# Decay input, sample rows and sample linear attention in plain fp32 over four column groups of TensorE

## The chip, the cores and the metric

One core of a Trainium2 chip runs the whole program. The metric is the device time of one execution in microseconds (us). TensorE is called PE (its weight loads PEld), VectorE DVE, ScalarE ACT, GpSimd POOL, and SyncE, which issues the DMAs, SP.

## The reference

One inference step of a decoder layer: a combined input projection feeds four heads of gated linear attention and a spatial-gating MLP, whose outputs share one output projection; a cross-attention over 256 memory tokens and a gated MLP with a causal convolution follow. There are 2048 prompt tokens and, beside them, 8 x 4 sample tokens that continue from a given state. All arrays are float32. The change touches the input projection and the linear attention:

```python
q, k, v, r, a, u, sv = split_cols(xn @ w_in)          # xn = rmsnorm(x, g_mix)
logg = log_sigmoid(a @ w_alpha + b_alpha) / 16        # a has 16 columns, logg 256
o, S = gla_chunked(q, k, v, logg, s0)                 # S_t = diag(exp(logg_t)) S_{t-1} + k_t^T v_t, o_t = q_t S_t
o = rmsnorm(o, g_gla_out) * silu(r)
sv = rmsnorm(gelu(sv), g_sgu)
```

## The kernel before

The prompt is worked in four blocks of 512 tokens (`s` is 0 to 3). The 32 sample tokens go through the mixer with block 1 (columns 512 to 543 of its tiles) and through the last MLP with block 2. `x` is kept with features on the partitions, in eight tiles `B.h[k]` of 128 x 544. A large product is done in three matmuls on split operands (`mm3`, lines 91 to 94): `split` makes of a fp32 tile a rounded part `hi` (ACT) and a remainder `lo` (DVE), both of the type fp32r, and the three products `hi hi`, `hi lo` and `lo hi` are summed in PSUM. `B.xs[k]` holds `hi` and `lo` of `x` times the gain `g_mix`; the scale of the norm (`B.xrs` by token, `B.xbc` broadcast) is applied when a result is taken from PSUM.

- `tm_steps` (line 674) makes products with tokens on the partitions: `sv` (profile name `t_ws`, line 816), `v` (`t_wv`) and `r` (`t_wr`). The eight feature tiles come in four weight units of two (step `j` = 0 to 3). In each step, each chunk `c` of 128 tokens takes six matmuls with the tokens as the stationary operand and 512 weight columns moving. In block 1 a fifth chunk holds the 32 sample tokens, also with 512 columns moving.
- `a_fn` (line 806) makes `a`, 16 columns wide, with features on the partitions: 16 matmuls of 32 stationary columns (`ap`, lines 812 and 813), on `wa1` (`hi` and `lo` of the weight side by side) and `wa2`. `gates` (line 900) multiplies it by `wal`, `w_alpha` twice and a row of `b_alpha` (`lgp`, plain fp32), and forms the log-sigmoid on ACT and DVE.
- `smp(p)` (line 1073) does the sample tokens' linear attention for a pair of heads: per head one matmul on the scores and eight on the given state (`ops`, lines 1079 and 1085), all summed in the same 32 PSUM rows; then `kvs` and the new state.
- `sample_steps` (line 1287) has a form that the change takes up: `sqp`, four plain fp32 matmuls of 32 stationary columns, each into another quarter of the PSUM partitions, and a product with `sum4` that adds the four quarters.

Weight tiles are loaded by `wload` into `wraw` tiles (five buffers), split into `whi` and `wlo` (five each), and asked for some five units ahead by `run`. What stands in which order on an engine is set by a scheduler when the program is built, from its own estimate of times; each engine then takes its instructions in that order. `acc` and `mps` are PSUM tiles, four buffers each.

Of the kernel before, what the change touches and what calls it, by code (L numbers as in the profile page):

```python
# [9 lines left out]
F32 = mybir.dt.float32  # L10
F32R = mybir.dt.float32r
# [26 lines left out]
def hymba_step_kernel(  # L38
# [31 lines left out]
    def acc(name):  # L70
        return accp.tile([128, 512], F32, tag="acc", name=name)
# [7 lines left out]
    def const(shape, name, dt=F32):  # L79
        return cp.tile(shape, dt, tag=name, name=name)  # L80
# [285 lines left out]
    pool.memset(sel[0:64, 0:1], 1.0)  # L366
    pool.memset(sel[64:128, 1:2], 1.0)

    cols_of = {}

    def load_cols(name, *vectors):
# [24 lines left out]
        nc.sync.dma_start(t, ap.partition_broadcast(128))  # L396
        return t

    wal = wa1 = wa2 = bsb = wsT = wss = None

    def late_constants():
        nonlocal wal, wa1, wa2, bsb, wsT, wss

        load_cols("b", ("gx", tiles_of(g_x)), ("gffn", tiles_of(g_ffn)),
                  ("cw", conv_w.rearrange("o j (k p) -> (o j k) p", p=128)), ("cb", tiles_of(conv_b)),
                  ("ggla", g_gla_out.rearrange("o h d -> (o h) d")), ("gsgu", g_sgu.rearrange("o h d -> (o h) d")))
        wal = const([33, 256], "wal")
        nc.sync.dma_start(wal[0:16, :], w_alpha[0])
        nc.sync.dma_start(wal[16:32, :], w_alpha[0])
        nc.sync.dma_start(wal[32:33, :], b_alpha)  # L410
        war = T_("war")
        war3 = war[:, :128].rearrange("p (k m) -> p k m", m=16)
        nc.sync.dma_start(war3, w_in[0, :, A0:A0 + 16].rearrange("(k p) m -> p k m", p=128))
        wa1 = const([128, 8, 32], "wa1", F32R)
        wa2 = const([128, 8, 32], "wa2", F32R)
        pool.memset(wa2[:, :, 16:32].bitcast(F32), 0.0)
        act.activation(wa1[:, :, 0:16], war3, AF.Copy)
        act.activation(wa2[:, :, 0:16], war3, AF.Copy)
        dve.tensor_tensor(wa1[:, :, 16:32], war3, wa1[:, :, 0:16].bitcast(F32), ALU.subtract)
# [12 lines left out]
        pool.tensor_copy(rep.rearrange("p (b i) -> p b i", i=4), ident[0:4, 0:4].unsqueeze(1).broadcast_to([4, 8, 4]))
        wss = const([NS, 4, NS], "wss")
        wssp = mps("wssp")
        pe.matmul(wssp[:NS, :16].rearrange("p (h i) -> p h i", h=4), rep, wsT[0:4, :, 0:4], start=True, stop=True)
        for h in range(4):
            dve.tensor_tensor(wss[:, h, :].rearrange("p (b i) -> p b i", i=4), blk3,
                              wssp[:NS, h * 4:(h + 1) * 4].unsqueeze(1).broadcast_to([NS, 8, 4]), ALU.mult)


        scd = state_conv[0].rearrange("b t f -> (b t) f")
        sctp = mps("sctp")
        for j in range(6):
# [229 lines left out]

    def tm_steps(w, m0, get_xs, sample, evac, name):

        ps = {}

        def fn(j, wu):
            xs = get_xs()
            wh, wl = wu  # L680
            for c in range(5 if sample else 4):
                n = 128 if c < 4 else NS
                cs = slice(c * 128, c * 128 + n)
                if j == 0:
                    ps[c] = acc(f"t_{name}{c}") if c < 4 else mps(f"t_{name}{c}")
                for kk in range(2):
                    k = 2 * j + kk
                    mm3(ps[c][:n], xs[k][0][:, cs], xs[k][1][:, cs], wh[:, kk], wl[:, kk], k == 0, k == 7)
                if j == 3:
                    evac(ps[c][:n], c, n)  # L690
        return [Step(lambda wu, j=j: fn(j, wu), [(w, 2 * j, 2, m0, 512, f"{name}{j}")]) for j in range(4)]

    def norm_in_steps(B):
# [81 lines left out]
    def proj_steps(B):  # L777
# [27 lines left out]

        def a_fn():
            B.aT = T_(f"aT{s}")
            pool.memset(B.aT[32:33, :T], 1.0)
            for ci, (c0, cw) in enumerate(chunks_of(sample)):
                ps = acc(f"ap{s}{ci}")  # L810
                for k in range(8):
                    pe.matmul(ps[:32, :cw], wa1[:, k], B.xs[k][0][:, c0:c0 + cw], start=k == 0, stop=False)
                    pe.matmul(ps[:32, :cw], wa2[:, k], B.xs[k][1][:, c0:c0 + cw], start=False, stop=k == 7)
                dve.tensor_tensor(B.aT[0:32, c0:c0 + cw], ps[:32, :cw], B.xbc[:32, c0:c0 + cw], ALU.mult)

        out = tm_steps(w, SV0, xs, sample, ev_tm("sv", lambda o, i, f: act.activation(o, i, AF.Gelu_apprx_tanh, scale=f)), f"ws{s}")
        out.append(Step(a_fn))
# [75 lines left out]
    def gla_steps(B):  # L893
# [6 lines left out]
        def gates():  # L900
            if sample:
                for p in range(2):
                    for i in range(2):
                        t = X(f"sg{p}{i}")
                        nc.sync.dma_start(t.rearrange("p (b v) -> p b v", b=4), sgd[:, 4 * i:4 * i + 4, p])
                        s0_of[p, i] = t
            lg = []
            for c2 in range(3 if sample else 2):
                n = 128 if c2 < 2 else NS
                wd = 512 if c2 < 2 else 256  # L910
                ps = mps(f"lgp{s}{c2}")
                for j in range(2 if c2 < 2 else 1):
                    c = 2 * c2 + j
                    pe.matmul(ps[:n, j * 256:(j + 1) * 256], B.aT[0:33, c * 128:c * 128 + n], wal, start=True, stop=True)
                t = T_(f"lgt{s}{c2}")
                act.activation(t[:n, :wd], ps[:n, :wd], AF.Abs)
                act.activation(t[:n, :wd], t[:n, :wd], AF.Exp, scale=-1.0)
                act.activation(t[:n, :wd], t[:n, :wd], AF.Ln, bias=1.0)
                o = U(f"lg{s}{c2}")
                dve.scalar_tensor_tensor(o[:n, :wd], ps[:n, :wd], 0.0, t[:n, :wd], ALU.min, ALU.subtract)  # L920
                lg.append(o[:, 0:256])
                if c2 < 2:
                    lg.append(o[:, 256:512])
            B.lg = lg
            B.P, B.qz, B.kt, B.eb, B.kms, B.b = {}, {}, {}, {}, {}, {}
# [147 lines left out]
        def smp(p):  # L1073
            s0 = [s0_of.pop((p, i)) for i in range(2)]
            ps = mps(f"ops{s}{p}")
            for hh in range(2):
                h = 2 * p + hh
                os_ = slice(hh * 128, (hh + 1) * 128)
                pe.matmul(ps[:NS, os_], B.P[h][:NS, SB:TM], B.v[4][:NS, h * 128:(h + 1) * 128], start=True, stop=False)
                qm = T_(f"qm{h}")  # L1080
                qm3 = qm[:, :256].rearrange("p (b i) -> p b i", b=8)
                pool.tensor_tensor(qm3, blkbc, B.qz[h][:, SB:TM].unsqueeze(1).broadcast_to([128, 8, NS]), ALU.mult)
                for bb in range(8):
                    sl = slice((bb % 4) * 128, (bb % 4 + 1) * 128)
                    pe.matmul(ps[:NS, os_], qm3[:, bb], s0[bb // 4][:, sl], start=False, stop=bb == 7)
            dve.tensor_copy(B.o[4][:NS, p * 256:(p + 1) * 256], ps[:NS, :256])
            for i in range(2):
                kv = mps(f"kvs{p}{i}")
                so = T_(f"so{p}{i}")
                for j in range(4):  # L1090
                    bb = 4 * i + j
                    sl = slice(j * 128, (j + 1) * 128)
                    for hh in range(2):
# [192 lines left out]

    def sample_steps():


        hr = [slice(h * NS, (h + 1) * NS) for h in range(4)]  # L1290

        def of_row(src, bb, name):

# [401 lines left out]
```

## Time and profile before

| | |
|---|---|
| median of three runs | 2878.52 us (2877.84 to 2882.15) |
| the profiled execution | 2882.3 us, its span 2880.3 us |
| PE busy | 2848.9 us |
| DVE, ACT, POOL busy | 1777.7, 1042.4, 615.6 us |
| moved by DMA | 625.47 MB, 217 GB/s over the span |
| mean granted clock of TensorE | 0.996 |

A row of a timeline gives the start, the duration, the engine and line, the output and inputs by the program's names, and how many instructions were merged into it; the duration of a matmul overlaps that of its neighbours, so what one occupies is read from the starts. One matmul in plain fp32 shows as two instructions. Rows of groups end with the busy time, the mean duration in ns, and the idle time ahead.

### The profile page before, as it was taken

How to read it: one execution, taken by the hardware profiler on the slowest of the kernel's cores; microseconds unless marked ns; L12 is line 12 of the kernel's file. 1: busy time of each engine (PE TensorE's matmuls, PEld its weight loads, DVE VectorE, ACT ScalarE, POOL GpSimd, SP SyncE). 2: the span in 40 equal slices, each digit the busy share in tenths (PEclk: the TensorE clock that was granted, in tenths of full speed). 3: DMA queues.
4: the chain of work that ended last, by engine and by line, in shares of the span. 5: the costliest groups of instructions: out<-in, count | busy, mean ns of one | idle time of the engine just before them, and what ended most of it. 6: DMA issues, size and time to landing. Idle time of an engine off the chain costs nothing.

```text
span 2880.3 us, 47363 instructions
## 1 busy us (share of the span) xinstructions
PE 2848.9 (99%) x18148; PEld 2519.9 (87%) x18148; DVE 1777.7 (62%) x3131; ACT 1042.4 (36%) x1890; POOL 615.6 (21%) x668
## 2 busy tenths in 40 slices
PE   8999999999999999999999999999999999999998
PEld 8888988887788898888888879899999888899998
DVE  7578468767657645555555773566666675474555
ACT  5635334333453423223124443422223533331221
POOL 1013112111112311222220221222221222132221
PEclk9999999999999999999999999999999999999999
DMA  9646579999932245877985214577776323567774
GB/s 311 203 151 219 186 252 328 332 325 339 341 105 61 66 141 186 303 273 277 326 313 200 74 45 165 195 256 260 258 265 213 106 66 106 191 249 266 275 283 177
DMA packets 359624, 625.47 MB, mean 217 GB/s; under 512 B 26683, under 2 KB 227326, under 8 KB 359400
## 3 DMA queue, kind: packets, MB, share of 16 engines
q1 hardware_dynamic: 359400, 622.46, 63.6%
q8 instruction: 144, 2.36, 0.3%
q14 instruction: 80, 0.66, 0.1%
HBM read 497.04 MB, written 125.31 MB: 216 GB/s over the span
## 4 chain that ended last, share of the span: by engine, by line
PE 89%; DVE 3%; DMA 3%; ACT 2%; issue 1%; POOL 1%; SPq 1%; DVEq 0%; POOLq 0%; ACTq 0%
PE d L92 5%; PE d L94 5%; PE d L93 5%; PE a_wo L92 2%; PE sc L94 2%; PE sc L93 2%; PE a_wo L93 2%; PE sc L92 2%; PE a_wo L94 2%; PE a_wx L94 2%; PE a_wx L93 2%; PE a_wx L92 2%; PE s L994 2%; PE t_wv L92 1%; PE t_wv L93 1%
## 5 line engine op out<-in xcount | busy, mean ns | idle before, releaser
L92 PE MATMUL d<-acth,whi_wd 128*128 128x512 f32 (+2 forms) x720 | 245.0, 340 | 0.1
L93 PE MATMUL d<-actl,whi_wd 128*128 128x512 f32 (+2 forms) x720 | 242.8, 337 | 0.0
L94 PE MATMUL d<-acth,wlo_wd 128*128 128x512 f32 (+2 forms) x720 | 242.8, 337 | 0.0
L1549 DVE TENSOR_TENSOR h<-d,h 128x512 f32<-128x512 f32 (+1 forms) x232 | 133.3, 581 | 145.0 <-PE d L94 144.8
L1488 POOL TENSOR_TENSOR c<-c,bc_f 128x512 f32<-128x512 f32 (+1 forms) x88 | 137.4, 1565 | 140.5 <-ACT c L1487 139.8
L94 PEld LDWEIGHTS d<-acth,wlo_wd 128*128 128x128 f32 x720 | 135.4, 188 | 15.7 <-issue 1.6
L92 PEld LDWEIGHTS d<-acth,whi_wd 128*128 128x128 f32 x720 | 135.5, 188 | 15.1 <-issue 1.2
L93 PEld LDWEIGHTS d<-actl,whi_wd 128*128 128x128 f32 x720 | 135.4, 188 | 14.6 <-issue 1.2
L1478 ACT ACTIVATE c<-g,colsb 128x512 f32<-128x512 f32 x88 | 71.7, 815 | 205.1 <-DVE g L1447 153.7
L94 PE MATMUL sc<-whi_qk,wol 128*128 128x256 f32 x512 | 144.4, 283 | 0.0
L92 PE MATMUL sc<-whi_qk,woh 128*128 128x256 f32 x512 | 144.1, 283 | 0.0
L93 PE MATMUL sc<-wlo_qk,woh 128*128 128x256 f32 x512 | 143.6, 282 | 0.0
L1510 POOL TENSOR_TENSOR c<-r_q_wup,c 128x512 f32<-128x512 f32 (+1 forms) x33 | 59.0, 1788 | 343.7 <-DVE r_q_wup L279 223.6
L1475 POOL COPY carry<-g 128x2 f32<-128x2 f32 x88 | 31.0, 353 | 435.3 <-DVE g L1447 433.2
L92 PE MATMUL a_wo<-ch,h_wo 128*128 128x512 f32 (+1 forms) x320 | 113.8, 359 | 5.4 <-DVE r L799 5.4
L987 POOL TENSOR_TENSOR e<-e,k 128x512 f32<-128x512 f32 (+1 forms) x48 | 69.2, 1442 | 223.6 <-DVE kr L983 160.9
L93 PE MATMUL a_wo<-cl,h_wo 128*128 128x512 f32 (+1 forms) x320 | 113.6, 356 | 0.2 <-POOL cl L85 0.2
L94 PE MATMUL a_wo<-ch,l_wo 128*128 128x512 f32 (+1 forms) x320 | 113.6, 355 | 0.0
L1479 DVE SCALAR_TENSOR_TENSOR c<-g,colsb,c 128x512 f32<-128x512 f32 x88 | 86.1, 978 | 30.5 <-ACT c L1478 30.0
L92 PE MATMUL a_wx<-pTh,whi_wx 128*128 128x512 f32 x256 | 101.0, 395 | 0.0
L93 PE MATMUL a_wx<-pTl,whi_wx 128*128 128x512 f32 x256 | 100.5, 393 | 0.0
L94 PE MATMUL a_wx<-pTh,wlo_wx 128*128 128x512 f32 x256 | 100.4, 392 | 0.0
(3355 smaller groups left out, 9463.6 us busy)
## 6 DMA issues: line engine op xcount, KB each, us to landing
whi_wd<-wd SPq DMA_DIRECT2D x66, 512.0 KB
wlo_wd<-wd SPq DMA_DIRECT2D x66, 512.0 KB
r_wo<-in_w_out_dram SPq DMA_DIRECT2D x32, 512.0 KB
whi_qk<-qkd SPq DMA_DIRECT2D x32, 512.0 KB
wlo_qk<-qkd SPq DMA_DIRECT2D x32, 512.0 KB
wlo_wx<-vod SPq DMA_DIRECT2D x32, 512.0 KB
whi_wx<-vod SPq DMA_DIRECT2D x32, 512.0 KB
r_wg<-in_w_gate_dram SPq DMA_DIRECT2D x22, 512.0 KB
```

The lines of the kernel that those rows point to most:

```text
L92: pe.matmul(ps, wh, xh, start=first, stop=False)
L93: pe.matmul(ps, wh, xl, start=False, stop=False)
L94: pe.matmul(ps, wl, xh, start=False, stop=last)
L987: pool.tensor_tensor(kl[:, :Tl], e[:, :Tl], B.k[p][:, :Tl], ALU.mult)
L994: pe.matmul(ps3[:, :, c * 64:(c + 1) * 64], kl[:, c * 128:(c + 1) * 128], kr3[:, :, c * 64:(c + 1) * 64], start=True, stop=True)
L1475: pool.tensor_copy(carry[:, f, :], g[:, SB:SB + 2])
L1478: act.activation(c[:, :SB], g[:, 2:SB + 2], AF.Identity, bias=cb, scale=w2)
L1479: dve.scalar_tensor_tensor(c[:, :SB], g[:, 1:SB + 1], w1, c[:, :SB], ALU.mult, ALU.add)
L1488: pool.tensor_tensor(c[:, :T], c[:, :T], B.fbc[:, :T], ALU.mult)
L1510: (dve, pool)[i].tensor_tensor(c[:, :T], q[i], c[:, :T], ALU.mult)
L1549: dve.tensor_tensor(B.h[m + mm][:, cs], ps[:, :cw], B.h[m + mm][:, cs], ALU.add)
```

## The change

1. The decay input `a` is made from `B.h` in plain fp32, feature tile `k` into column group `k % 4` (eight matmuls instead of 16); an ACT copy of all 128 rows replaces the scaled DVE copy, the sum over the four groups falls to `lgp` (`wal` now holds `w_alpha` four times), and the scale by token and the bias follow in a new DVE operation ahead of the log-sigmoid.
2. The sample rows of `sv`, `v` and `r` are made from the unsplit weights `raw` and `sxg` (sample columns of `x` times `g_mix`), four feature tiles at a time, each in its column group; after `j == 3` ACT copies the 128 x 512 result and one product with `sum4` adds the groups. The raw tile of a step is kept until that burst.
3. In `smp` the eight state products of a head go to four column groups; `ot` and `opt` add them.

```diff
+    hr = [slice(g * NS, (g + 1) * NS) for g in range(4)]
+    sxg = const([128, 8 * NS], "sxg")
...
-        wal = const([33, 256], "wal")
-        nc.sync.dma_start(wal[0:16, :], w_alpha[0])
-        nc.sync.dma_start(wal[16:32, :], w_alpha[0])
-        nc.sync.dma_start(wal[32:33, :], b_alpha)
+        wal = const([128, 256], "wal")
+        pool.memset(wal, 0.0)
+        for g in range(4):
+            nc.sync.dma_start(wal[g * NS:g * NS + 16, :], w_alpha[0])
+        bal = bvec(b_alpha.rearrange("o c -> (o c)"), 256, "bal")
...
+        wa = const([128, 8, 32], "wa")
+        pool.memset(wa, 0.0)
+        for k in range(8):
+            dve.tensor_scalar(wa[:, k, 0:16], war3[:, k], gcol("gmix", k), None, ALU.mult)
...
+        def spread(j):
+            if j == 1:
+                ps["q"] = mps(f"t_{name}q")
+            for k, raw in held:
+                pe.matmul(ps["q"][hr[k % 4]], sxg[:, k * NS:(k + 1) * NS], raw, start=j == 1, stop=j == 3)
+            held.clear()
+            if j == 3:
+                ps["t"] = T_(f"t_{name}t")
+                act.activation(ps["t"][:, :512], ps["q"], AF.Copy)
...
-            for c in range(5 if sample else 4):
+            if sample:
+                held.extend((2 * j + kk, raw[:, kk]) for kk in range(2))
+                if j % 2:
+                    spread(j)
+            for c in range(4):
...
+            if sample and j == 3:
+                ps[4] = mps(f"t_{name}4")
+                pe.matmul(ps[4][:NS], sum4, ps["t"][:, :512], start=True, stop=True)
+                evac(ps[4][:NS], 4, NS)
...
+            if sample:
+                dve.tensor_scalar(sxg[:, k * NS:(k + 1) * NS], B.h[k][:, SB:TM], gcol("gmix", k), None, ALU.mult)
...
                 for k in range(8):
-                    pe.matmul(ps[:32, :cw], wa1[:, k], B.xs[k][0][:, c0:c0 + cw], start=k == 0, stop=False)
-                    pe.matmul(ps[:32, :cw], wa2[:, k], B.xs[k][1][:, c0:c0 + cw], start=False, stop=k == 7)
-                dve.tensor_tensor(B.aT[0:32, c0:c0 + cw], ps[:32, :cw], B.xbc[:32, c0:c0 + cw], ALU.mult)
+                    pe.matmul(ps[hr[k % 4], :cw], wa[:, k], B.h[k][:, c0:c0 + cw], start=k < 4, stop=k >= 4)
+                act.activation(B.aT[:, c0:c0 + cw], ps[:, :cw], AF.Copy)
...
-                act.activation(t[:n, :wd], ps[:n, :wd], AF.Abs)
+                o = U(f"lg{s}{c2}")
+                for j in range(wd // 256):
+                    js = slice(j * 256, (j + 1) * 256)
+                    dve.scalar_tensor_tensor(o[:n, js], ps[:n, js], B.xrs[:n, 2 * c2 + j:2 * c2 + j + 1], bal[:n],
+                                             ALU.mult, ALU.add)
+                act.activation(t[:n, :wd], o[:n, :wd], AF.Abs)
...
-                    pe.matmul(ps[:NS, os_], qm3[:, bb], s0[bb // 4][:, sl], start=False, stop=bb == 7)
-            dve.tensor_copy(B.o[4][:NS, p * 256:(p + 1) * 256], ps[:NS, :256])
+                    pe.matmul(ps[hr[bb % 4], os_], qm3[:, bb], s0[bb // 4][:, sl], start=0 < bb < 4, stop=bb >= 4)
+            ot = T_(f"ot{p}")
+            dve.tensor_copy(ot[:, :256], ps[:, :256])
...
+            ps = mps(f"opt{s}{p}")
+            pe.matmul(ps[:NS, :256], sum4, ot[:, :256], start=True, stop=True)
+            dve.tensor_copy(B.o[4][:NS, p * 256:(p + 1) * 256], ps[:NS, :256])
```

The scheduler orders the program anew. On PE, in block 1's product `v`, the sample chunk of the first weight unit stood before like this (`t_wv_8610` is its PSUM tile, `xh` and `xl` the split `x`):

```order
L94 MATMUL t_wv_8596<-h_wv_8140,xl_1_7810 128x512
L92 MATMUL t_wv_8610<-h_wv_8140,xh_0_7805 32x512
L93 MATMUL t_wv_8610<-l_wv_8141,xh_0_7805 32x512
L92 MATMUL t_wv_8603<-h_wv_8140,xh_0_7805 128x512
```

and the same place has now, up to the second weight unit (`t_wv1q` is the PSUM tile of the four groups):

```order
L685 MATMUL t_wv1q<-r_wv_8136,sxg 32x512
L92 MATMUL t_wv_8591<-h_wv_8138,xh_0_7809 128x512
L93 MATMUL t_wv_8591<-l_wv_8139,xh_0_7809 128x512
L94 MATMUL t_wv_8591<-h_wv_8138,xl_0_7810 128x512
L92 MATMUL t_wv_8591<-h_wv_8138,xh_1_7814 128x512
L93 MATMUL t_wv_8591<-l_wv_8139,xh_1_7814 128x512
L94 MATMUL t_wv_8591<-h_wv_8138,xl_1_7815 128x512
L685 MATMUL t_wv1q<-r_wv_8136,sxg 32x512
L685 MATMUL t_wv1q<-r_wv_8251,sxg 32x512 x2
```

The sample matmuls moved out of the chunks into four new ones, of which one stands apart from the other three. On PE at the end of block 1's linear attention, ahead of its output projection, stood before:

```order
L1085 MATMUL ops_9566<-sg_8390,qm_9579 32x128 x4
L1085 MATMUL ops_9566<-sg_8392,qm_9579 32x128 x4
L1095 MATMUL kvs_9590<-v_8819,km_9456 64x128 x2
L1095 MATMUL kvs_9605<-v_8819,km_9457 64x128 x2
L865 MATMUL zp_9656<-wsT,sv_8150 128x128
```

and now stands:

```order
L1115 MATMUL ops_9539<-sg_8375,qm_9552 32x128 x4
L1126 MATMUL kvs_9564<-v_8799,km_9436 64x128 x2
L1126 MATMUL kvs_9579<-v_8799,km_9437 64x128 x2
L1133 MATMUL opt_9594<-ot_9562,sum_151 32x256
L685 MATMUL t_wr1q<-r_wr_8777,sxg 32x512 x2
L685 MATMUL t_wr1q<-r_wr_8995,sxg 32x512 x2
L685 MATMUL t_wr1q<-r_wr_9001,sxg 32x512 x2
L685 MATMUL t_wr1q<-r_wr_9231,sxg 32x512 x2
```

All eight sample matmuls of `r` moved behind the linear attention, so that its four raw weight tiles `r_wr` are in use up to there. On SP's queue the loads of the output projection's weights (`r_wo`) stood before:

```order
L102 DMA r_wo_9257<-in_w_out_dram 128x4x256
L102 DMA r_wo_9477<-in_w_out_dram 128x4x256
L102 DMA r_wo_9620<-in_w_out_dram 128x4x256
L857 DMA gsgub<-in_g_sgu_dram 32x512
L859 DMA out_dram<-svo 32x512
L102 DMA r_wo_9671<-in_w_out_dram 128x4x256
```

and now stand:

```order
L102 DMA r_wo_9237<-in_w_out_dram 128x4x256
L883 DMA gsgub<-in_g_sgu_dram 32x512
L885 DMA out_dram<-svo 32x512
L1131 DMA out_dram<-so_8963 128x4x128
L1376 DMA kc_12122<-in_cache_mem_k_dram 128x512
L1131 DMA out_dram<-so_8978 128x4x128
L1376 DMA kc_12124<-in_cache_mem_k_dram 128x512
L102 DMA r_wo_9457<-in_w_out_dram 128x4x256
```

The second of these loads moved behind two state outputs, and it and the three after it now each wait for the split of the load before.

More of the change, by code (lines that the diff above doesn't have):

```diff
@@ L397, in bvec @@
         return t
-    wal = wa1 = wa2 = bsb = wsT = wss = None
+    wal = wa = bal = bsb = wsT = wss = None
     def late_constants():
-        nonlocal wal, wa1, wa2, bsb, wsT, wss
+        nonlocal wal, wa, bal, bsb, wsT, wss
         load_cols("b", ("gx", tiles_of(g_x)), ("gffn", tiles_of(g_ffn)),
@@ L413, in late_constants @@
         nc.sync.dma_start(war3, w_in[0, :, A0:A0 + 16].rearrange("(k p) m -> p k m", p=128))
[L414 to L419, printed above, removed]
+        wa = const([128, 8, 32], "wa")
+        pool.memset(wa, 0.0)
+        for k in range(8):
+            dve.tensor_scalar(wa[:, k, 0:16], war3[:, k], gcol("gmix", k), None, ALU.mult)
         bsb = bvec(b_s.rearrange("o h i -> (o h i)"), 512, "bsb")
@@ L676, in tm_steps, with unit, load @@
         ps = {}
+        held = []
+        def spread(j):
[7 more added lines that the diff above has]
+                act.activation(ps["t"][:, :512], ps["q"], AF.Copy)
         def fn(j, wu):
             xs = get_xs()
-            wh, wl = wu
-            for c in range(5 if sample else 4):
-                n = 128 if c < 4 else NS
-                cs = slice(c * 128, c * 128 + n)
+            raw, wh, wl = wu
+            if sample:
[3 more added lines that the diff above has]
+            for c in range(4):
+                cs = slice(c * 128, (c + 1) * 128)
                 if j == 0:
-                    ps[c] = acc(f"t_{name}{c}") if c < 4 else mps(f"t_{name}{c}")
+                    ps[c] = acc(f"t_{name}{c}")
                 for kk in range(2):
                     k = 2 * j + kk
-                    mm3(ps[c][:n], xs[k][0][:, cs], xs[k][1][:, cs], wh[:, kk], wl[:, kk], k == 0, k == 7)
+                    mm3(ps[c], xs[k][0][:, cs], xs[k][1][:, cs], wh[:, kk], wl[:, kk], k == 0, k == 7)
                 if j == 3:
-                    evac(ps[c][:n], c, n)
-        return [Step(lambda wu, j=j: fn(j, wu), [(w, 2 * j, 2, m0, 512, f"{name}{j}")]) for j in range(4)]
+                    evac(ps[c], c, 128)
+            if sample and j == 3:
+                ps[4] = mps(f"t_{name}4")
+                pe.matmul(ps[4][:NS], sum4, ps["t"][:, :512], start=True, stop=True)
+                evac(ps[4][:NS], 4, NS)
+        def unit(j):
+            def load():
+                raw = wload(w, 2 * j, 2, m0, 512, f"{name}{j}")
+                return raw, *wsplit(raw, f"{name}{j}")
+            return load
+        return [Step(lambda wu, j=j: fn(j, wu), [unit(j)]) for j in range(4)]
     def norm_in_steps(B):
@@ L807, in a_fn @@
             B.aT = T_(f"aT{s}")
-            pool.memset(B.aT[32:33, :T], 1.0)
             for ci, (c0, cw) in enumerate(chunks_of(sample)):
@@ L913, in gates @@
                     c = 2 * c2 + j
-                    pe.matmul(ps[:n, j * 256:(j + 1) * 256], B.aT[0:33, c * 128:c * 128 + n], wal, start=True, stop=True)
+                    pe.matmul(ps[:n, j * 256:(j + 1) * 256], B.aT[:, c * 128:c * 128 + n], wal, start=True, stop=True)
                 t = T_(f"lgt{s}{c2}")
-                act.activation(t[:n, :wd], ps[:n, :wd], AF.Abs)
+                o = U(f"lg{s}{c2}")
[4 more added lines that the diff above has]
+                act.activation(t[:n, :wd], o[:n, :wd], AF.Abs)
                 act.activation(t[:n, :wd], t[:n, :wd], AF.Exp, scale=-1.0)
                 act.activation(t[:n, :wd], t[:n, :wd], AF.Ln, bias=1.0)
-                o = U(f"lg{s}{c2}")
-                dve.scalar_tensor_tensor(o[:n, :wd], ps[:n, :wd], 0.0, t[:n, :wd], ALU.min, ALU.subtract)
+                dve.scalar_tensor_tensor(o[:n, :wd], o[:n, :wd], 0.0, t[:n, :wd], ALU.min, ALU.subtract)
                 lg.append(o[:, 0:256])
@@ L1287, in sample_steps @@
     def sample_steps():
-        hr = [slice(h * NS, (h + 1) * NS) for h in range(4)]
         def of_row(src, bb, name):
```

## The prediction

> **What bounds the kernel now.** I read the page's busy table and chain first, then who TensorE (PE) waits for, then the stretches around block 1, which alone carries the 32 sample tokens.
>
> ```profile
> span 2880.3 us, 47363 instructions
> PE 2848.9 (99%) x18148; PEld 2519.9 (87%) x18148; DVE 1777.7 (62%) x3131; ACT 1042.4 (36%) x1890; POOL 615.6 (21%) x668
> PE 89%; DVE 3%; DMA 3%; ACT 2%; issue 1%; POOL 1%; SPq 1%; DVEq 0%; POOLq 0%; ACTq 0%
> ```
>
> PE is busy 2848.9 of 2880.3 us, so 31 us idle are left in the whole program, and 89% of the chain that ended last is PE. A matmul row taken from PE's queue shortens the span unless a wait opens in its place. The waits say where that is nearest:
>
> ```profile
> PE a_wo L92 <- DVE r L799: 5.4, 3, 2.2
> PE s L994 <- POOL e L987: 4.6, 4, 1.5
> 970.00:980.00 10.00, 10.00 (x77) 7.69 (x77) 5.65 (x11) 7.46 (x27) 5.19 (x3) 1.00 0.63 211
> 980.00:990.00 10.00, 8.65 (x63) 6.92 (x61) 6.80 (x18) 1.91 (x6) 6.57 (x5) 0.69 0.16 47
> 990.00:1000.00 10.00, 9.83 (x64) 9.32 (x64) 8.78 (x28) 5.91 (x10) 1.34 (x1) 0.80 0.20 60
> ```
>
> The first two rows are the longest recurring waits. The other rows are stretches (columns: PE, PEld, DVE, ACT, POOL busy, granted clock, DMA share, GB/s). Just ahead of block 1's out projection (`a_wo`) PE is idle 1.35 us of ten, and the clock falls to 0.69 and 0.80. Elsewhere in block 1 PE is full.
>
> **The prices.** A matmul's own duration overlaps its neighbours', so I price by start to start. First what goes:
>
> ```profile
> 805.40 0.39 PE L92 MATMUL t_ws<-h_ws,xh 128*32 128x512 f32 x1
> ...
> 806.79 0.38 PE L1589 MATMUL yp<-ident,h 128*128 128x128 f32 x2
> 106.70:110.45 3.75, 3.73 (x16) 1.64 (x16) 0.00 (x0) 1.00 1.07 352
> 822.36:826.44 4.08, 4.08 (x32) 3.47 (x32) 0.00 (x0) 1.00 0.27 68
> 976.45 1.94 PE L1085 MATMUL ops<-sg,qm 128*32 128x128 f32 x16
> 978.31 0.40 PE L1079 MATMUL ops<-v,P 32*32 32x128 f32 x2
> 978.64 1.93 PE L1085 MATMUL ops<-sg,qm 128*32 128x128 f32 x16
> 980.51 0.65 PE L1095 MATMUL kvs<-v,km 32*64 32x128 f32 x8
> ```
>
> - Sample rows of the token-major products: six split matmuls run from 805.40 to 806.79, 1.39 us, so the 24 of one product take 5.56 and the three products (`ws`, `wv`, `wr`) 16.7 us.
> - Decay input `ap`: 16 matmuls of 512 columns in 3.73 us in each of three blocks, and 32 of 272 columns in 4.08 in block 1: 15.3 us.
> - State term `ops`: 978.31 minus 976.45, and 980.51 minus 978.64, is 1.86 and 1.87 per head, four heads: 7.5 us.
>
> Removed: 39.5 us. What comes instead is plain fp32 over four column groups. The trace has that form (`sqp`, a sample projection), and it has plain fp32 over the full array (`lgp`); each fp32 matmul shows as two instructions:
>
> ```profile
> 1160.55 0.28 PE L93 MATMUL a_wup10S<-wul,wup10A 128*128 128x256 f32 x1
> 1160.67 0.28 PE L94 MATMUL a_wup10S<-wuh,wup10A 128*128 128x256 f32 x1
> 1160.88 1.07 PE L1311 MATMUL sqp<-r_sq,smpx 128*32 128x256 f32 x16
> 1161.88 0.39 PE L92 MATMUL a_wg11A<-w,wg11A 128*128 128x256 f32 x1
> 1162.10 0.29 PE L93 MATMUL a_wg11A<-w,wg11A 128*128 128x256 f32 x1
> 1162.23 0.28 PE L94 MATMUL a_wg11A<-w,wg11A 128*128 128x256 f32 x1
> 126.29 1.99 PE L914 MATMUL lgp<-wal,aT 33*128 33x256 f32 x8
> 128.21 0.50 PE L92 MATMUL a_wq<-xh,h_wq 128*128 128x512 f32 x1
> ```
>
> Four `lgp` matmuls of 256 columns take 1.92 us, 0.48 each. Eight `sqp` matmuls of 256 take 1.00 us, 0.125 each: the groups run side by side, 3.84 times faster. Around such a burst the start to start grows from 0.12 to 0.21 and from 0.13 to 0.22, so a burst costs 0.18 more at its edges; I take 0.2. Four neighbours of 512 columns stream what eight of 256 do: 1.0 us. One that stands alone takes 0.96.
>
> The Trainium skill, page "TensorE: Matmul & The Clock Gate", section "Measured speedup vs the span model", measured 3.07 for four tiles (packed by rows). Our trace has 3.84 for four column groups and decides; by 3.07 the 20.0 us of bursts below (edges apart) would be 25.0, an estimate.
>
> The Trainium skill, page "TensorEngine Tiling (Array Packing)", section "Key Properties", says that changing the tiling mode drains TensorE. That speaks against scattered bursts, and by it every piece pays; the rows agree, at 0.09 us per edge.
>
> **What is added on PE.**
> - Products: `ws` comes in two bursts of four, 2.0 us. `wv` stands in the order as one alone plus three, twice: 2 x (0.96 + 1.0) = 3.9. `wr` is one burst of eight, 2.0. Seven pieces of edges, 1.4. Each product ends with a 512-column fp32 sum over the groups, 0.96 plus edge 0.1: 3.2. Together 12.5 us.
> - `ap`: two blocks 2.0 each; block 3, where a transpose splits one off, 3.0; block 1 has 16 of 272 columns, 16 x 272 / 2048 = 2.1. Edges of five pieces 1.0. Together 10.1.
> - `ops`: 16 of 128 columns per pair of heads are 2048 columns, 1.0 us if the streaming limits; if one instruction cannot follow another faster than in `sqp` (16 in 1.00 us), 32 take 2.0. I take the middle, 1.5, since no row has this form at 128 columns; two pairs 3.0 (ends 2.0 and 4.0). Two 256-column sums, 0.48 + 0.1 each: 1.2. Together 4.2.
>
> Added 26.8, removed 39.5: PE's queue gets 12.7 us shorter. `lgp` streams the same 256 columns with 128 rows instead of 33 at the same start to start, so I price it at zero.
>
> **What is added elsewhere.** The decay's scale and bias move behind `lgp`: 17 vector operations of 128x256. The nearest row:
>
> ```profile
> L983 DVE SCALAR_TENSOR_TENSOR kr<-e,sel,q 128x256 f32<-128x256 f32 x104 | 46.4, 485 | 19.3 <-ACT e L975 15.9 <-ACT e L977 2.6 <-DMA out_dram<-so 0.8
> 840.00:850.00 10.00, 10.00 (x73) 9.14 (x72) 6.05 (x19) 9.76 (x14) 0.00 (x0) 1.00 0.36 106
> 20.00:30.00 10.00, 10.00 (x88) 10.00 (x87) 5.14 (x9) 4.65 (x8) 0.00 (x0) 1.00 1.13 302
> ```
>
> 8.2 us on DVE, some two per block, beside 96 queued `a_wq` matmuls that stand between `lgp` and its reader (840 to 850: PE full, DVE 60%). Cost zero; without that cover it would be the 2 us of a block. ACT is at 98% there, and takes the two `aT` copies from DVE; they stand before `lgp`, covered by `a_wk`. The eight scalings for `sxg` and the copies `t`, `ot` are under 1 us each and have matmuls queued behind them. At the start two DMAs more and a 128 KB broadcast of the bias enter a saturated stretch (20 to 30: DMA share 1.13, 302 GB/s), 0.4 us, while PE is full: between 0 and 1, I take 0.4.
>
> **The loads behind it.** A raw weight tile is now kept until the burst that reads it, instead of until its split. In `wr` all four are kept to the end, so of five buffers one is left, and the next loads (`r_wo`, on SP's queue) go through it one after the other: each waits for the split of the one before.
>
> ```profile
> 919.63 0.38 SPq L102 DMA_DIRECT2D r_wo<-in_w_out_dram  x1
> 920.50:921.00 0.50, 0.50 (x6) 0.50 (x6) 0.48 (x2) 0.00 (x0) 0.00 (x0) 1.00 0.47 70
> 922.00:922.50 0.50, 0.50 (x7) 0.48 (x6) 0.50 (x3) 0.02 (x1) 0.00 (x0) 1.00 0.96 338
> L84 ACT ACTIVATE h_wo<-r_wo x8: 1046/1058/1062, 935.8 to 1012.9; 128x1024 fp32r<-128x1024 f32 x8
> L85 DVE TENSOR_TENSOR l_wo<-r_wo,h_wo x8: 1202/1224/1227, 938.0 to 1014.0; 128x1024 fp32r<-128x1024 f32 x8
> ```
>
> A lone 512 KB load goes from 919.63 to 922.5, 2.9 us; with the splits 1.06 and 1.22 one turn takes 5.2. Four turns after the first split (938.0) end by 960, and `a_wo` starts at 988.9, so PE never lacks the weights. But ACT and DVE take instructions in order, and the splits now stand between the `e`, `kh` and `o` steps of the linear attention: each of four may hold them up by up to the 2.9 us of a load. I expect most of it covered by `t_wr` matmuls and take 1 us, ends 0 and 11.6.
>
> **The end of block 1.** The burst of `wr` (2.2), `opt` and the last sum come where PE idles 1.35 us, between `ops` and `a_wo`; I give 1 us back for that, ends 0 and 1.35. They also need PSUM buffers there.
>
> Sum: -12.7 + 0.4 + 1 - 1 = -12.3 us. On the profiled execution, 2882.3 us (span 2880.3), that is 2870.0; this execution lies 3.8 above the median of the three runs shown, 2878.52, so I predict 2866.2 us.
>
> **Rivals.**
> 1. Clock kept. These rows show where it halves:
>
> ```profile
> 988.90 0.57 PE L92 MATMUL a_wo<-ch,h_wo 128*128 128x272 f32 x1 [1.09 <-DVE r L799]
> 989.27 0.43 PE L93 MATMUL a_wo<-cl,h_wo 128*128 128x272 f32 x1
> ...
> 994.22 0.29 PE L92 MATMUL a_wo<-ch,h_wo 128*128 128x272 f32 x1
> 994.35 0.29 PE L93 MATMUL a_wo<-cl,h_wo 128*128 128x272 f32 x1
> ```
>
> The matmuls follow at 0.23 us until 994, then at 0.13. With dense bursts in the stretch before, the drop may not come: about half of the 5.2 us from 988.9, 2.6, and 1.5 from the `zp` ahead of it. Result -12.3 - 4.1 = -16.4, 2862. Against it: the waits ahead of `a_wo` (1.09) stay.
> 2. The splits hold up block 1's chain: with 7 to 11.6 us exposed instead of 1 the result is -6 to -2, about 2875. For it: DVE and ACT are in order; against it: DVE is only 57% busy at 970 to 980.
> 3. Slower: the column groups do not run side by side with 512 columns. The place is every burst. The bursts without their edges are 7.9 + 9.1 + 3.0 = 20.0 us; without overlap their 24 + 24 matmuls of 512 columns cost 0.96, the 16 of 272 0.51 and the 32 of 128 0.24, together 61.9, and the sum becomes +30, 2908. It decides from 20.0 + 12.3 = 32.3 us on, bursts 1.6 times as long as priced. Against it: `sqp`, same form, half the columns.
> 4. The overlap lies between: where the groups' streams hinder each other at 512 columns, bursts of 25 instead of 20 us give -7.3, 2871. `sqp` speaks against it, but at 256 columns. (That is the overlap of the Trainium skill's page "TensorE: Matmul & The Clock Gate", section "Measured speedup vs the span model"; no run here shows it.)
>
> **How the numbers follow.** Main case (-9 to -15) 55%; clock kept (-15 to -20) 13%; overlap between, or part of rival 2 (-6 to -9) 15%; rival 2 in full (within 6 us) 11%; slower by over 6 us 6%, half of it rival 3. 0.2%, 5.8 us, is what a measurement tells from no change. Faster 0.83, same 0.11, slower 0.06. The range goes from 2858, just beyond the clock case, to 2875, into rival 2; outside lie the slower cases and half of rival 2 above, and little below, some 14% in all.
>
> **What would show it.** `t_ws` of 128*32 with fp32r gone, `t_ws1q` in bursts of 1.0 us per four; `ap` near 2.0 us instead of 3.73; `ops` near 1 to 2 us per pair of heads instead of 3.7; PE's busy time shorter by some 12 us, its idle time near 31. Wrong: `t_wr1q` over 4 us, PE waits on `P`, `kh` or `o` in block 1, or a start of `a_wo` later than 12 us ahead of 988.9.

## The result and the profile after

The changed kernel takes 2865.24 us (median of five, 2863.78 to 2871.47) against 2879.53 us before (2877.84 to 2882.15): ratio 0.995, 95% interval 0.994 to 0.9961. The prediction was 2866.2 us, range 2858 to 2875, and a change of -12.3 us; measured are -14.3 us, with the interval -17.3 to -11.2. The sum came out near, but its gains and two of its losses were priced too low, as the profile shows. Two executions far off the others, 3739.79 us of the kernel before and 6203.86 us of `light_start`, are left out of the ratios below. The profiled execution after took 2871.47 us (span 2869.5), the slowest of the five. From its page: span, PE's busy time, the chain's shares.

```profile
span 2869.5 us, 47351 instructions
PE 2834.5 (99%) x18134; PEld 2504.1 (87%) x18134; DVE 1784.4 (62%) x3160; ACT 1044.4 (36%) x1896; POOL 613.9 (21%) x665
PE 91%; DVE 3%; ACT 2%; issue 1%; POOL 1%; DMA 1%; SPq 0%; DVEq 0%; POOLq 0%; ACTq 0%
```

From the list of what PE waited for (total us, times, longest):

```profile
PE a_wo L92 <- DVE r L827: 4.3, 2, 2.2
PE bp L960 <- DVE lg L950: 3.8, 2, 2.2
PE mkt L567 <- DVE mkf L558: 2.8, 2, 1.9
```

PE is busy 14.4 us less than before, where 12.7 were priced. But its idle time grew from 31.4 to 35.0 us. The wait of block 1's `a_wo` for `r` (1.09) is gone, and in its place stand two waits that before did not have: `bp`, the running sum of the decay `lg` and the next matmul after `a_wq`, waits for `lg`, and at the start `mkt`, which transposes the keys `mkf` of the memory tokens, waits for `mkf`.

The matmuls, from PE's timeline after (start, duration, ..., how many):

```profile
109.59 1.92 PE L839 MATMUL ap<-h,wa 128*32 128x512 f32 x16
111.44 0.98 PE L589 MATMUL wqp<-ident,r_wqf 128*128 128x128 f32 x7
112.19 0.47 PE L92 MATMUL a_wk<-xh,h_wk 128*128 128x512 f32 x1
...
127.09 1.89 PE L940 MATMUL lgp<-wal,aT 128*128 128x256 f32 x8
128.63 0.58 PE L92 MATMUL a_wq<-xh,h_wq 128*128 128x512 f32 x1
...
799.77 1.07 PE L685 MATMUL t_ws1q<-r_ws,sxg 128*32 128x512 f32 x8
800.76 0.50 PE L92 MATMUL t_ws<-h_ws,xh 128*128 128x512 f32 x1
...
909.04 0.65 PE L1115 MATMUL ops<-sg,qm 128*32 128x128 f32 x16
909.62 0.40 PE L1109 MATMUL ops<-v,P 32*32 32x128 f32 x2
909.95 0.64 PE L1115 MATMUL ops<-sg,qm 128*32 128x128 f32 x16
910.52 0.65 PE L1126 MATMUL kvs<-v,km 32*64 32x128 f32 x8
```

Four sample matmuls of 512 columns take 0.99 us (799.77 to 800.76; a fp32 matmul shows as two instructions). `ap` of block 0 takes 1.85. One head's eight state matmuls take 0.57 or 0.58, a third of the 1.86 before. `lgp` on 128 rows takes 1.54 from its start to `a_wq`; on 33 rows it took 1.92.

The new wait in block 1. Before, on PE and DVE, the same `lg` ended at 851.05, with `bp` at 854.01, so that 3.0 us of slack were left:

```profile
854.01 1.05 PE L930 MATMUL bp<-tri,lg 128*128 128x128 f32 x8
850.04 1.01 DVE L920 SCALAR_TENSOR_TENSOR lg<-lgp,lgt 128x512 f32<-128x512 f32 x2 [3.50 <-ACT lgt L918]
```

On PE, DVE and ACT after:

```profile
848.51 0.60 PE L960 MATMUL bp<-tri,lg 128*128 128x128 f32 x4
851.32 0.72 PE L960 MATMUL bp<-tri,lg 128*128 128x128 f32 x4 [2.20 <-DVE lg L950]
...
838.97 0.47 DVE L945 SCALAR_TENSOR_TENSOR lg<-lgp,xrs,bal 128x256 f32<-128x256 f32 x1
839.37 1.20 DVE L85 TENSOR_TENSOR l_wv<-r_wv,h_wv 128x1024 fp32r<-128x1024 f32 x1
840.50 1.64 DVE L945 SCALAR_TENSOR_TENSOR lg<-lgp,xrs,bal 128x256 f32<-128x256 f32 x4
850.57 0.69 DVE L950 SCALAR_TENSOR_TENSOR lg<-lg,lgt 128x512 f32<-128x512 f32 x1 [3.50 <-ACT lgt L949]
...
841.00 0.63 ACT L947 ACTIVATE lgt<-lg 128x512 f32<-128x512 f32 x1 [5.89 <-DVE lg L945]
841.65 1.28 ACT L948 ACT_TABLE_LOAD   x1
```

`lgp` is done by 836.4. The new operation (L945) comes to its turn on DVE at 838.97 and 840.50, behind scalings of `sv` and a weight split. ACT, which before began on `lgp` directly, waits 5.89 us for it. Four changes of ACT's function table (1.28 us each, as in the last row) and the log-sigmoid follow. PE meanwhile arrives earlier, for its queue is shorter.

The start, on SP's queue and DVE before, then on both after:

```profile
19.85 0.38 SPq L102 DMA_DIRECT2D r_wk<-in_wk_x_dram  x1
...
23.68 0.42 DVE L557 TENSOR_TENSOR mkf<-mkp,mbcs 128x256 f32<-128x256 f32 x1
```

```profile
19.76 2.95 SPq L447 DMA_DIRECT2D sc<-in_state_conv_dram  x1
22.80 0.38 SPq L102 DMA_DIRECT2D r_wk<-in_wk_x_dram  x1
...
24.55 1.20 DVE L420 TENSOR_SCALAR wa<-war,colsa 128x16 f32<-128x16 f32 x8 [4.28 <-DMA war<-in_w_in_dram]
25.66 0.42 DVE L558 TENSOR_TENSOR mkf<-mkp,mbcs 128x256 f32<-128x256 f32 x1
```

With the added loads ahead of it the weight load of 19.85 is issued at 22.80; 1.0 us of this stands already at the weight load before it (17.48 against 16.48), the rest arises at the loads between the two. DVE stands 4.28 us at the eight operations that make `wa`, with `mkf` behind them, 2.0 us later than before.

The end of block 1 after, as stretches (PE, PEld, DVE, ACT, POOL busy, granted clock, DMA share, GB/s) and then on PE's timeline:

```profile
970.00:980.00 10.00, 9.67 (x61) 5.93 (x54) 5.99 (x16) 2.79 (x8) 5.96 (x5) 0.74 0.88 281
980.00:990.00 10.00, 10.00 (x74) 9.58 (x73) 9.13 (x28) 6.49 (x11) 1.83 (x2) 0.92 0.10 35
```

```profile
979.19 0.60 PE L92 MATMUL a_wo<-ch,h_wo 128*128 128x272 f32 x1
979.59 0.43 PE L93 MATMUL a_wo<-cl,h_wo 128*128 128x272 f32 x1
981.74 0.29 PE L93 MATMUL a_wo<-cl,h_wo 128*128 128x272 f32 x1
```

The clock still halves, but by the trace's record of the clock it stands at half (granted clock 0.5) for 6.83 us (from 974.8) instead of 10.24 (from 983.8), and `a_wo` is at full pace 2.5 us after its start instead of 5.2.

### The profile page after: what moved, and what is told of

It reads as the page before. It is cut to its first block, busy times and chain, and to the rows that moved or that the text cites. A ratio compares the mean times of both kernels' runs of the same rounds, so it can differ in the third digit from the quotient of the medians.

```text
span 2869.5 us, 47351 instructions
## 1 busy us (share of the span) xinstructions
PE 2834.5 (99%) x18134; PEld 2504.1 (87%) x18134; DVE 1784.4 (62%) x3160; ACT 1044.4 (36%) x1896; POOL 613.9 (21%) x665
## 4 chain that ended last, share of the span: by engine, by line
PE 91%; DVE 3%; ACT 2%; issue 1%; POOL 1%; DMA 1%; SPq 0%; DVEq 0%; POOLq 0%; ACTq 0%
PE d L92 6%; PE d L94 6%; PE d L93 6%; PE a_wo L92 2%; PE sc L94 2%; PE sc L93 2%; PE a_wo L93 2%; PE a_wo L94 2%; PE sc L92 2%; PE a_wx L93 2%; PE a_wx L94 2%; PE a_wx L92 2%; PE s L1024 2%; PE a_wg L94 1%; PE a_wup L94 1%
## 5 line engine op out<-in xcount | busy, mean ns | idle before, releaser
L92 PEld LDWEIGHTS d<-acth,whi_wd 128*128 128x128 f32 x720 | 135.3, 188 | 15.3 <-issue 1.2
L93 PEld LDWEIGHTS d<-actl,whi_wd 128*128 128x128 f32 x720 | 135.5, 188 | 14.4 <-issue 1.2
L1017 POOL TENSOR_TENSOR e<-e,k 128x512 f32<-128x512 f32 (+1 forms) x48 | 72.7, 1514 | 237.1 <-DVE kr L1013 137.0
```

The lines of the kernel that those rows point to most:

```text
L92: pe.matmul(ps, wh, xh, start=first, stop=False)
L93: pe.matmul(ps, wh, xl, start=False, stop=False)
L1017: pool.tensor_tensor(kl[:, :Tl], e[:, :Tl], B.k[p][:, :Tl], ALU.mult)
```

## The experiments

Each kernel ran four to eleven times against the kernel before, `one_group` twice. "Block 1" is the time on PE from the last `d` of the block before (the last product of its MLP) to the first `sc` behind block 1 (the scores of its cross-attention), in the profiled execution; "first `t_ws`" is when block 0's first product starts.

| kernel | ratio to before (95%) | block 1, us | first `t_ws`, us | half clock at the end of block 1, us |
|---|---|---|---|---|
| before | 1 | 251.1 | 70.3 | 10.2 |
| after | 0.995 (0.994 to 0.9961) | 241.4 | 74.1 | 6.8 |
| after_again | 0.9951 (0.9938 to 0.9963) | 239.9 | 72.5 | 6.8 |
| only_ap | 0.9995 (0.9986 to 1.0003) | 250.8 | 71.8 | 6.8 |
| only_tm | 0.9969 (0.9959 to 0.998) | 244.2 | 70.3 | 3.4 |
| only_smp | 0.9996 (0.9987 to 1.0005) | 249.3 | 70.6 | 10.2 |
| no_ap | 0.9958 (0.9944 to 0.9971) | 239.5 | 70.2 | 6.8 |
| scale_first | 0.9928 (0.9916 to 0.9941) | 236.3 | 72.3 | 0 |
| light_start | 0.9955 (0.9941 to 0.9968) | 238.9 | 69.8 | 0 |
| both_mended | 0.9927 (0.9914 to 0.9939) | 236.2 | 70.5 | 0 |
| one_burst | 0.9946 (0.9933 to 0.996) | 236.9 | 72.6 | 0 |
| ap_mended | 0.9967 (0.9955 to 0.998) | 249.3 | 70.1 | 10.2 |
| one_group | 1.0098 (1.008 to 1.0116) | 264.2 | 72.7 | 6.8 |
| best | 0.9915 (0.9901 to 0.9928) | 232.9 | 70.0 | 0 |

**after_again**: the changed kernel a second time.

> The changed kernel once more, for a second profile. Theory A (the losses come with the change): the first t_ws of block 0 starts again 3 to 4 us later than in the kernel before (70.34 us there), and bp waits again some 2 us for lg in blocks 1 and 2. Rival (they were accidents of one execution, 6 us above the median): the start is within 1 us of before's, or the waits for lg are gone. Time 2863 to 2868 by both.

Measured 2867.61 us. Waits of PE, and the first `t_ws`:

```profile
PE bp L960 <- DVE lg L950: 3.8, 2, 2.2
PE mkt L567 <- DVE mkf L558: 2.5, 2, 1.7
```

```profile
72.53 0.50 PE L92 MATMUL t_ws<-h_ws,xh 128*128 128x512 f32 x1
```

Both losses are there again. They come with the change, though the late start is 2.2 us here and not 3.7. The first profile has 3.41 us of half clock at 36.1 us, which this one has not; half of that, 1.7 us, is about the difference.

**The three parts alone.** `only_ap` has the first part of the change, `only_tm` the second, `only_smp` the third, each put on the kernel before (the diff of the change, cut at those places).

> The kernel before with the decay input alone changed (ap in column groups, lgp on 128 rows, scale and bias behind lgp, the new constants). Theory A (by the rows of the profile after: ap -6.7, lgp -1.5, the late start +2.7, the waits of bp for lg +4.7): -0.8 us, so no difference from before that can be measured. Rival (as priced in the prediction: ap -5.2, start +0.4, lg covered): -4.8 us.

> The kernel before with the sample rows of the three products alone changed. Theory A (by the rows after: sv -2.1, v +0.3, r -2.3, and the half clock at the end of block 1 shorter, -1.7): -5.8 us, with no late start and no wait of bp for lg. Rival 1 (as priced, the clock as before): -4.1 us. Rival 2 (the raw tiles kept stall the loads): within 1 us of before, with waits of a_wo or t_wr for weights.

> The kernel before with the state term of the sample's linear attention alone changed. Theory A (by the rows after, 0.57 us for the eight matmuls of a head): -4.5 us. Rival (as priced, 1.5 us per pair): -3.3 us. With the waits of z and r at the end of block 1 left as they are, part of the second pair's gain may be lost there: -2 to -3 us.

Measured: -0.05, -0.31 and -0.04% (of 2881.51 us: -1.4, -8.9 and -1.2); their sum, -0.40%, lies near the whole change's -0.49%. The sample rows carry the change: 6.9 of their 8.9 us (interval -11.8 to -5.8) are block 1, more than either number expected, and rival 2 is excluded. The decay input is worth nothing that can be told from zero as written (interval -4.0 to +0.9), which is theory A. In `only_ap` the waits of PE are those of the whole change:

```profile
PE bp L932 <- DVE lg L922: 3.8, 2, 2.2
PE mkt L566 <- DVE mkf L557: 1.4, 2, 1.2
```

`only_smp` stays short of both numbers, -4.5 and -3.3, though its interval, -3.7 to +1.4, excludes only the first; the last sentence, some of the second pair's gain lost at the end of block 1, comes closest. A wait of PE there, the stretch, and the start of `a_wo`:

```profile
PE a_wo L93 <- POOL cl L85: 0.8, 1, 0.8
```

```profile
980.00:990.00 10.00, 7.65 (x32) 6.94 (x32) 7.99 (x22) 5.28 (x8) 3.97 (x3) 0.57 0.39 104
```

```profile
981.60 0.57 PE L92 MATMUL a_wo<-ch,h_wo 128*128 128x272 f32 x1 [1.42 <-DVE r L800]
```

Block 1 has gained 4.6 us when `a_wo` starts (192.5 us from the last `d`, 789.09, against 197.1 before). PE waits 1.42 there for `r`, then 0.82 for `cl`, and the half clock lasts 10.24 us again, but nearly all of it falls on `a_wo`, whereas before half had passed when `a_wo` began. At the end of block 1 1.8 of the 4.6 us are left.

**no_ap**: the second and third part without the first.

> The changed kernel without its first part: sample rows and state term changed, decay input as before. Theory A (the state term's gain is lost where it stands alone, to a_wo's waits for r and cl at the end of block 1, and is kept where the burst and the sum of r stand there): -8.9 us of the sample rows alone and -4 more, -13 us, some 0.9955 of before. Rival (the state term is worth its lone 1.2 us): -10 us, 0.9965.

Measured -0.42%, -12.1 us (interval -16 to -8), between the two, nearer to theory A. In its profile `a_wo` of block 1 does not wait for `r` at all. That the burst and the sum of `wr` fill the time in which `r` becomes ready fits this, but the timing does not separate the theories.

**scale_first**: scale and bias ahead of `lgp` again, so that ACT and DVE read `lgp` directly as before; the 17 operations behind it are gone.

```diff
-                act.activation(B.aT[:, c0:c0 + cw], ps[:, :cw], AF.Copy)
+                dve.tensor_tensor(B.aT[:, c0:c0 + cw], ps[:, :cw], B.xbc[:, c0:c0 + cw], ALU.mult)
+            pool.memset(B.aT[0:1, :T], 1.0)
...
```

Row 0 of `aT` is the row of ones, and row 0 of `wal` the bias, for which the start has one more load; `w_alpha` moves to rows 1 to 16 of each group.

> The changed kernel with the decay's scale and bias back ahead of lgp (the scaled DVE copy of ap, with a row of ones for the bias), its start left as it is. Theory A (the two or four operations per block behind lgp set the waits of bp): the waits of bp for lg go, block 1 gains 2.7 and block 2 2.0 us against the changed kernel: -4.7 us, some 2861 us, ratio to before about 0.9935. Rival (the chain to lg is late for another reason, such as the splits queued on DVE): bp still waits 1.5 us or more and the time stays within 1.5 us of the changed kernel's.

Measured 2858.99 us, 0.9928. No wait of `bp` for `lg` is left in its list. PE and DVE of block 1:

```profile
846.69 1.05 PE L958 MATMUL bp<-tri,lg 128*128 128x128 f32 x8
842.70 1.01 DVE L948 SCALAR_TENSOR_TENSOR lg<-lgp,lgt 128x512 f32<-128x512 f32 x2 [3.50 <-ACT lgt L946]
```

`lg` is done at 843.7, 3.0 us ahead of `bp`. Against `after_again` block 1 gains 2.5 and block 2 1.9 us at this place (from the last `a_wq` to the last `bp`), 4.3 of the 4.7 expected. Theory A holds. The time fell by more, 6 to 9 us, but the ratios leave almost 4 us to each side; the half clock at the end of block 1 is absent too in this execution. `a_wo` waits there again, 0.35 us for `r` and 0.92 for `cl`, as it does in `light_start` and `both_mended`: 1.3 us that the changed kernel does not have.

**light_start**, and **both_mended** with the two edits together:

```diff
-        for g in range(4):
-            nc.sync.dma_start(wal[g * NS:g * NS + 16, :], w_alpha[0])
-        bal = bvec(b_alpha.rearrange("o c -> (o c)"), 256, "bal")
+        nc.sync.dma_start(wal[0:16, :], w_alpha[0])
+        for g in range(1, 4):
+            pool.tensor_copy(wal[g * NS:(g + 1) * NS, :], wal[0:NS, :])
...
-        for k in range(8):
-            dve.tensor_scalar(wa[:, k, 0:16], war3[:, k], gcol("gmix", k), None, ALU.mult)
+        pool.tensor_tensor(wa[:, :, 0:16], war3, cols_of["gmix"][:, 0:8].unsqueeze(2).broadcast_to([128, 8, 16]), ALU.mult)
```

In `light_start` the load of `bal` stands in `a_fn` of block 0; `both_mended` has none, and the rows of its `wal` and `wa` are those of `scale_first`.

> The changed kernel with a lighter start: one load of w_alpha and three copies on POOL in place of four loads, the 128 KB of the bias asked for with block 0's ap instead of at the start, and wa made by one POOL operation instead of eight on DVE. Theory A (the late start is the queue of loads, and DVE held by war): the first t_ws of block 0 starts within 1 us of before's 70.34, -1.5 to -3 us against the changed kernel, 2863 us. Rival (another delay of the start): the first t_ws again 2 us or more later, time as the changed kernel's.

> Both of these edits together, without the broadcast bias. Theory A: the sum, -6 to -8 us against the changed kernel, 2858 to 2861 us, ratio to before 0.9925. Rival (the time saved comes back as waits at the end of block 1, or at other places): -2 to -4 us.

That the late start comes from these lines is shown by the first `t_ws`: 71.8 to 74.1 us in the kernels with the loads and `wa` as the change has them, 69.8 to 70.6 in all others. In `light_start`, against the 72.53 of `after_again` above, it and the load of `bal` on SP's queue are:

```profile
69.81 0.50 PE L92 MATMUL t_ws<-h_ws,xh 128*128 128x512 f32 x1
```

```profile
14.29 0.33 SPq L398 DMA_DIRECT2D bal<-in_b_alpha_dram  x1
```

The load of the bias did not move to block 0: it is issued at 14.29 us, among the loads of the start, for the scheduler put it there. The start is as early as before all the same, so this load is not what made it late. Which share belongs to the loads of `w_alpha` and which to DVE's turn at `wa` is not shown, since both were changed at once.

In the profiles the 1.85 us between `scale_first` and `both_mended` at this place stay, as 1.7, until 1833 us, where a half clock of 3.41 us, which the other execution does not have, takes 1.5 of them back. The timings do not show the gain: 0.9955 against 0.9951 (a median of 2868.03 us where 2863 was expected), and 0.9927 against 0.9928. So the late start is a loss of about 2 us in the trace, and below what these timings separate. The -6 to -8 us expected of `both_mended` hold (2859.46 us against 2865.24 and 2867.61; by the ratios -6.6 to -6.9), but by the timings it is `scale_first` that brings them.

**one_burst**: all eight sample matmuls of a product behind the fourth weight unit.

```diff
-                if j % 2:
+                if j == 3:
                     spread(j)
...
```

> The changed kernel with all eight sample matmuls of each product in one burst after the fourth weight unit, so that four raw tiles are held in every product. Theory A (only bursts and edges count, the loads have slack): 2.5 to 2.7 us off the products sv and v, some 2864 us. Rival (raw tiles that are kept hold the loads back): waits of PE for split weights in block 1, time equal to or above the changed kernel's.

Measured 0.9946 against 0.9951, less than expected and not separable. Block 1 is 3.0 us shorter than in `after_again`, but next to nothing of that (0.1) stands at the first pair's `ops` (906 us), where the execution has spent a half clock of 3.41 us from 849.9 on; the rest comes at the end, where no half clock came. No wait of PE for split weights appeared, though four raw tiles were held in each product, so the raw buffers do not bound this stage.

**one_group**: every fp32 matmul of the change into the first column group, same count, no groups side by side.

> The changed kernel with every fp32 matmul of the three parts in the first column group alone (the sums over groups then take 32 rows). Theory A (what pays is that four groups run side by side): the prediction's arithmetic without overlap, bursts of 61.9 instead of 20.0 us, so +42 us against the changed kernel, about 2908 us, slower than before. Rival (the groups do little, fewer instructions do it): within 5 us of the changed kernel.

Measured 2909.13 us. `ap` of block 0:

```profile
108.19 7.05 PE L839 MATMUL ap<-h,wa 128*32 128x512 f32 x16
115.18 0.98 PE L589 MATMUL wqp<-ident,r_wqf 128*128 128x128 f32 x7
```

6.99 us instead of 1.85, 3.8 times as long. Without overlap the change loses 1%, and the total agrees with what was worked out beforehand to about 1 us. In part this is chance: single bursts are 8 to 9% shorter than priced (`ap` 6.99 instead of 8 x 0.96 = 7.68, four sample matmuls 3.55 instead of 3.84), so some of the +42 us come from elsewhere, which was not traced. The rival of this run, that the groups do little, is excluded.

**ap_mended**: the decay input alone, with scale first and light start, on the kernel before; **best**: both mended and the single burst.

> The kernel before with the decay input alone changed, but scale and bias ahead of lgp and the light start. Theory A (the part was worth nothing only for its waits and its start): -1.4 as measured alone, -4.3 for the waits of bp, -1.8 for the start: -7.5 us, 0.9974 of before. Rival (what it saves is lost elsewhere in any form): -1 to -3 us.

> Both mended, and all eight sample matmuls of a product in one burst. Theory A (the gains add): -1 to -2 us against both_mended (0.9927 of before), so 0.9920 to 0.9924, 2857 to 2858 us. Rival (the end of block 1 waits for r or cl, or raw tiles run short): 0.9927 or above.

`ap_mended` measured -0.33%, -9.5 us (-13 to -6): the part that was worth nothing as written is worth as much as the sample rows once nothing waits on it. `best` measured 2855.60 us, 0.9915, a little better than expected (0.9920 to 0.9924 lie within its interval), the fastest kernel here. What PE waits for `r` in `best` (before: three times, 5.4 us), and the start of its `a_wo` in block 1:

```profile
PE a_wo L92 <- DVE r L826: 4.3, 2, 2.2
```

```profile
967.68 0.39 PE L92 MATMUL a_wo<-ch,h_wo 128*128 128x272 f32 x1
967.91 0.29 PE L93 MATMUL a_wo<-cl,h_wo 128*128 128x272 f32 x1
968.04 0.29 PE L94 MATMUL a_wo<-ch,l_wo 128*128 128x272 f32 x1
```

`a_wo` begins without a wait and, from its second matmul on, at 0.13 us spacing, the full clock. With the single burst of `wr` and its sum just ahead of `a_wo`, the 1.3 us of waits that `both_mended` has there are gone (`one_burst` has none either).

## Why the prediction was right, and where it was not

- **Products** (16.7 removed, 12.5 added). Held. In `only_tm` block 1 is 6.9 us shorter; the half clock there is 6.8 us shorter, worth about half of that, which leaves 3.5 of the 4.2. PE also waits 0.6 us longer at `a_wo` there (0.29, 0.54 and 1.02 us against 1.09 and 0.17), which accounts for the rest. Bursts of four take 0.99 as priced; the burst of `wr` stayed near 2.1 us.
- **`ap`** (15.3 to 10.1). Better: from its start to the next `a_wk` blocks 0 to 3 save 1.9, 2.1, 1.9 and 0.8, together 6.7 instead of 5.2. The edge of 0.2 is not paid beside the plain fp32 transposes that stand next to it (109.59 to 111.44 is 1.85, less than the 2.0 taken for the burst alone).
- **`lgp`**, priced at zero: 0.4 us less in three of the four blocks, as in the rows above.
- **`ops`** (7.5 to 4.2). Better: each pair saves 2.58 us (909.70 to 914.09 before, 908.71 to 910.52 after, with the score matmuls), less 0.55 for a sum. So 32 instructions of 128 columns take 1.15 us, near the lower end that was taken from streaming.
- **The operations behind `lgp`, cost zero**: the step that failed. The prediction looked at DVE's busy share (60%) and at the matmuls that cover the chain. What counted was the turn of each operation in DVE's queue, and that ACT's chain, four table changes long, began only behind it. It cost 2.5 and 1.9 us in blocks 1 and 2, 4.3 in all, near the 2 us of a block that the text gave for the case without cover, and none in blocks 0 and 3.
- **The start, 0 to 1 us**: failed too. It is about 2 us. DMA share and a busy PE were the wrong rows; the queue of SP and DVE's turn at `wa` were the right ones.
- **The raw buffer chain** (+1, rival 2): it formed and cost nothing. From SP's and ACT's queue after:

```profile
935.45 29.83 SPq L102 DMA_DIRECT2D r_wo<-in_w_out_dram  x5
954.13 1.06 ACT L84 ACTIVATE h_wo<-r_wo 128x1024 fp32r<-128x1024 f32 x1 [4.61 <-DMA r_wo<-in_w_out_dram]
962.35 1.06 ACT L84 ACTIVATE h_wo<-r_wo 128x1024 fp32r<-128x1024 f32 x1 [2.85 <-PE t_wr L94]
```

  ACT does stand 4.61 us at a load, but PE waits for none of what is behind it, and the last split is over 14 us ahead of `a_wo`.
- **The end of block 1** (-1, rival 1). The wait of 1.09 went, and the half clock lasted 6.8 us in both profiles of the changed kernel: part of rival 1. A sign of being wrong that the prediction named did come: `a_wo` starts 9.7 us ahead of 988.9 and not 12, since `bp` and the start had taken their part by then. Nor did PE's idle time stay near 31 us (35.0).
- **Rivals 3 and 4**: bursts of four in 0.99 us exclude both; `one_group` shows what rival 3 would have been.

PE's queue gave some 3 us more than priced, and two covers that were taken for free cost 6 us, of which 0.4 was in the sum; the end of block 1 returned 2.8 (the wait of 1.09 and half of 3.41 us of half clock, an estimate) where 1 was counted, and the 1 us for the raw buffers was not needed. Added up anew this gives -12.5 us, against -12.3 predicted: the errors cancel. The timings moved by -14.3, so some 2 us are not accounted for, within the interval of -17.3 to -11.2. That the predicted 2866.2 us lies within 1 us of the measured 2865.24 is luck for another reason too: the median of before was 2878.52 us of three runs for the prediction, and 2879.53 of five in the result. The mechanisms on PE were right; that the total is so close owes much to chance.

## What to carry to other kernels

An operation added on a half-idle engine is free only if it gets its turn in time: look at what stands ahead of it in that engine's queue, at the chain behind it, and at how much earlier the shortened engine will now ask for the result. Keep a cheap scaling where queued matmuls cover it (here ahead of a small matmul) rather than inside the chain to the next consumer. When a change in several parts moves less than its queue arithmetic says, time the parts alone: one part here was worth nothing that could be measured until its two waits were taken away, and 9.5 us (6 to 13) after.

## What was not expected of the hardware

- A group of eight plain fp32 instructions with 128 rows is 0.38 us shorter, up to the next matmul, than one with 33 rows (1.54 against 1.92 us; with 32 rows, in `one_group`, 1.92 again). The spacing inside the groups is the same, 0.216 us from start to start; the difference lies at the two edges of the group. The first `a_wq` behind the group starts 0.03 instead of 0.31 us after the last `lgp`.
- The stretches of half clock in all these traces last 3.41, 6.83 or 10.24 us, except at the program's end. After the same wait of 2.20 us for `lg` one execution of the changed kernel has one (851.9 us) and another has none, and one cost 1.5 us in `both_mended`, so executions of one kernel differ by a few us. In each trace the stretches start whole multiples of 3.413 us apart (239, 36, 211, 44 and 154 of them in the first profile after), so on a grid of windows, which lies differently from one execution to the next. The wait of 2.20 us lies within one window in the first profile, and half clock follows; in `after_again` it falls into two windows as 1.23 and 0.96 us, and none follows. Over all 14 traces, from 30 us on, half clock followed each of the 20 windows in which PE was idle for more than 1.9 us. It followed less idle time only at the end of block 1 and at 1826 to 1875 us, and why is open; elsewhere up to 1.89 us of idle in a window went without it. The Trainium skill, page "TensorE: Matmul & The Clock Gate", section "What's actually happening", gives a free-running window of 3.4 us and says that the number of slow matmuls varies from run to run; the durations and the changing places agree.
- The 1.09 us wait at `a_wo` and the low clock there belong together in the kernels without the sample rows' change (6.8 to 10.2 us of half clock in four of four); with it there were 0 to 6.8, and none in three kernels where `a_wo` waits 0.35 and 0.92 us. PE's idle time does not explain it: 0.26 us in the window ahead of the half clock before, beside many small matmuls (`ops`, `kvs`). Why some executions had none stays open.
